# Merge and output projection: merge inputs one merge ahead, w_o by column halves, four token tiles at once

## The chip, the cores and the metric

The kernel runs as one launch on one core of one Trainium2 chip. The metric is the device time in microseconds, the median of three runs. Engines are named as in the profile: PE (matrix), DVE (vector), ACT (scalar), POOL (GpSimd), SP (which issues most DMAs). A difference of 0.2% (about 5 us) is what a measurement of this kernel can tell from none.

## The reference

One encoder block on 1024 tokens of width 1024 in float32: adaptive norm, an input projection, an attention branch and a state-space (SSD) branch, a gated merge, an output projection and a feed-forward block. The part that the change touches is

```python
merged = sigmoid(g_attn) * (attn @ w_attn_out) + sigmoid(g_ssd) * (ssd @ w_ssd_out)   # ssd is RMS-normed, D_INNER = 2048
x = x + gate1 * (merged @ w_o)                                                        # 1024 x 1024
h2 = rms_norm(x, norm2_w) * (1.0 + scale2) + shift2
```

## The kernel before

Each float32 factor is split into a high and a low part (`split`: ACT casts the high part, DVE subtracts to get the low part), and a product is three matmuls of 128 x 128 by 128 x 512 for each block of 128 along the contraction (high by high, high by low, low by high). Every engine works through a fixed list of instructions in order; the order is set by a scheduler when the kernel is built, and semaphores hold an instruction until its inputs and its buffer are ready.

Two stages matter here. In the first (`p5` in the code), the SSD output is multiplied by `w_so`, one row block `i` of 128 output features at a time. The contraction over 2048 is cut into two halves of 8 blocks: the first half of row blocks 6 and 7 (`HELD = 2`) stays in PSUM (`part`), that of the others was computed earlier and lies in DRAM (`s_d`, read back as `e_s`). So the list of jobs is (6, first), (7, first), then the second half for 6, 7, 0, 1, 2, 3, 4, 5. A job has two units, one for each half of the tokens (512 columns), of 24 matmuls into a PSUM tile `psg` (six buffers). After each unit of a second job comes a merge: it loads the attention output `e_a`, the two gates `e_ga` and `e_gs`, and `e_s`; ACT takes the sigmoid of both gates, POOL multiplies `e_a` by `e_ga` and `e_gs` by the norm `rbc`, DVE adds `psg` to `e_s` (this frees the PSUM buffer), multiplies by `e_gs`, adds `e_a`, and the sum is split into `mh` (ACT) and `ml` (DVE). All four input tiles have two buffers (`bufs=2`). The weights `wraw`, `whi`, `wlo` of a job have two buffers too, so they are loaded and split one job ahead. The merges are named here by row block and half, in their order (6,0), (6,1), (7,0), ... (5,0), (5,1).

In the second stage (`p6`), `w_o` is loaded as eight row blocks of 512 KB (`woraw`, four buffers, so that the last four are loaded only when the first four are split), split into `woh` and `wol`, which take the buffers of the SSD operands `g2h`/`g2l` (tag "mrg") that the last job still reads. Then, for each of eight tiles of 128 tokens and each half of the 1024 columns, 24 matmuls over the blocks k = 0 to 7 add into a PSUM tile `pso` (tag "ps2", four buffers that lie where the `psg` buffers lay), DVE multiplies by `gate1` and adds `x`, and ACT takes the sum of squares. The weights of the feed-forward part (`wop` splits) are prepared in between.

Of the kernel before, what the change touches and what calls it, by code (L numbers as in the profile page):

```python
# [89 lines left out]
def block(ctx: ExitStack, tc: tile.TileContext, ia, out, upto=99, dbg=None):  # L90
# [1154 lines left out]
    def load_wo():  # L1245
        raw = wop.tile([P, D], F32, name="woraw", tag="woraw", bufs=4)
        k = len(wo_raw)
        dma(raw, w_o[k * P:(k + 1) * P, :])
        wo_raw.append(raw)

    g2hi, g2lo = mrg_tiles("g2")
    with tc.tile_pool(name="p5", bufs=1, reuse_waits="tile") as p5, \
# [3 lines left out]
        order = list(range(KT - HELD, KT)) + list(range(KT - HELD))  # L1256
# [37 lines left out]
        for n, (i, second) in enumerate(jobs):  # L1294
# [25 lines left out]
    whi, wlo = mrg_tiles("wo")  # L1320
# [27 lines left out]
    with tc.tile_pool(name="p6", bufs=1, reuse_waits="tile") as p6:  # L1348
        gate1 = p6.tile([P, D], F32, name="gate1")
        dma(gate1, g_d[0].partition_broadcast(P))  # L1350
        for k in range(KT):
            if k >= 4:
                load_wo()
            for half in range(2):
                split(whi[k][half], wlo[k][half], wo_raw[k][:, half * 512:(half + 1) * 512])
# [10 lines left out]

        for t in range(NT):
            th, sl = t // 4, slice((t % 4) * P, (t % 4 + 1) * P)
            x1[t] = p6.tile([P, D], F32, name="x1", tag="x1", bufs=5)
            ss2 = p6.tile([P, 2], F32, name="ss2", tag="ss2", bufs=2)  # L1370
            for n in range(2):
                ns = slice(n * 512, (n + 1) * 512)
                xr = p6.tile([P, 512], F32, name="xr", tag="xr", bufs=2)
                dma(xr, x_in[t * P:(t + 1) * P, ns])
                ps = ps7.tile([P, 512], F32, name="pso", tag="ps2", bufs=4)
                for k in range(KT):
                    T.matmul(ps, mhi[k][th][:, sl], whi[k][n], start=k == 0, stop=False)
                    T.matmul(ps, mhi[k][th][:, sl], wlo[k][n], start=False, stop=False)
                    T.matmul(ps, mlo[k][th][:, sl], whi[k][n], start=False, stop=k == KT - 1)
                tt(V, x1[t][:, ns], ps, gate1[:, ns], ALU.mult)  # L1380
                tt(V, x1[t][:, ns], x1[t][:, ns], xr, ALU.add)
                A.activation(xr, x1[t][:, ns], AF.Square, accum_out=ss2[:, n:n + 1])
# [412 lines left out]
```

## Time and profile before

| what | value |
| --- | --- |
| three runs | 2495.03, 2496.18, 2498.93 us, median 2496.18 us |
| the profiled execution | 2497.45 us, its span 2495.7 us, so 1.75 us lie outside the span |
| granted clock of PE over the span | 0.985 |
| busy share of the span | PE 96%, PE weight load 77%, DVE 69%, ACT 44%, POOL 35% |

A busy share is an average over all stages. The two stages above take the stretch from about 1616 to 1840 us of the span. The clock has two levels, 1.2 and 2.4 GHz, and is given as a share of the higher.

### The profile page before, as it was taken

How to read it: one execution, taken by the hardware profiler on the slowest of the kernel's cores; microseconds unless marked ns; L12 is line 12 of the kernel's file. 1: busy time of each engine (PE TensorE's matmuls, PEld its weight loads, DVE VectorE, ACT ScalarE, POOL GpSimd, SP SyncE). 2: the span in 40 equal slices, each digit the busy share in tenths (PEclk: the TensorE clock that was granted, in tenths of full speed). 3: DMA queues.
4: the chain of work that ended last, by engine and by line, in shares of the span. 5: the costliest groups of instructions: out<-in, count | busy, mean ns of one | idle time of the engine just before them, and what ended most of it. 6: DMA issues, size and time to landing. Idle time of an engine off the chain costs nothing. (4 is left out here: it accounts for less than half of the span.)

```text
span 2495.7 us, 32129 instructions
## 1 busy us (share of the span) xinstructions
PE 2393.4 (96%) x11275; PEld 1916.6 (77%) x11275; DVE 1717.7 (69%) x2293; ACT 1096.2 (44%) x1880; POOL 872.2 (35%) x672
## 2 busy tenths in 40 slices
PE   5899999999999999999899999998998999999999
PEld 5898777888867777777667767776777888788887
DVE  5756346777756666666577797556569887767794
ACT  5454522555556666666333343344232222364430
POOL 2311107666511111110356676424018766114200
PEclk9999999999999999999999999999999999999999
DMA  7654661333531213111676776466315544554522
GB/s 261 192 160 135 203 215 60 92 100 110 178 126 57 85 52 89 56 57 47 207 215 208 216 221 185 146 225 213 112 51 194 189 145 165 214 184 134 156 82 87
DMA packets 282161, 363.36 MB, mean 146 GB/s; under 512 B 33673, under 2 KB 166513, under 8 KB 282001
## 3 DMA queue, kind: packets, MB, share of 16 engines
q1 hardware_dynamic: 209841, 285.22, 36.7%
q10 hardware_dynamic: 72160, 76.11, 9.1%
q8 instruction: 89, 1.46, 0.3%
q14 instruction: 71, 0.58, 0.1%
HBM read 248.18 MB, written 113.06 MB: 145 GB/s over the span
## 5 line engine op out<-in xcount | busy, mean ns | idle before, releaser
L891 DVE TENSOR_REDUCE nm<-pss 128x1 f32<-128x1024 f32 x128 | 156.7, 1225 | 133.6 <-PE pss L889 132.1
L379 PE MATMUL psq<-twl,hh 128*128 128x400 f32 (+1 forms) x512 | 193.0, 379 | 6.2 <-DVE twl L153 6.2
L378 PE MATMUL psq<-twh,hh 128*128 128x400 f32 (+1 forms) x512 | 192.3, 381 | 3.3 <-ACT qkvr L511 1.2
L380 PE MATMUL psq<-twh,hl 128*128 128x400 f32 (+1 forms) x512 | 192.0, 377 | 0.0
L893 ACT ACTIVATE pf<-pss,nm 128x1024 f32<-128x1024 f32 x128 | 143.2, 1119 | 101.7 <-PE pst L904 99.0
L153 DVE TENSOR_TENSOR pl<-pst,ph 128x512 fp32r<-128x512 f32 x256 | 167.9, 683 | 27.8 <-ACT ph L167 27.8
L904 PEld LDWEIGHTS pst<-masks,pf 128*128 128x128 f32 x1024 | 118.4, 140 | 69.9 <-issue 29.6
L167 ACT CAST ph<-pst 128x512 fp32r<-128x512 f32 x256 | 146.5, 586 | 54.0 <-PE pst L904 40.8
L904 PE MATMUL pst<-masks,pf 128*128 128x128 f32 x1024 | 157.0, 276 | 11.7 <-DVE pl L153 9.7
L1673 PE MATMUL p<-o,o 128*128 128x512 f32 x400 | 155.3, 389 | 0.5 <-DVE o L153 0.5
L1672 PE MATMUL p<-o,o 128*128 128x512 f32 x400 | 153.7, 390 | 1.9 <-DVE ac L153 1.4
L153 POOL TENSOR_TENSOR av<-av,rz 64x512 f32<-64x512 f32 x32 | 41.0, 1283 | 326.2 <-DMA rz<-rz 154.9
L1674 PE MATMUL p<-o,o 128*128 128x512 f32 x400 | 153.7, 389 | 0.0
L713 DVE SCALAR_TENSOR_TENSOR tap<-pad,cwT,tap 128x1024 f32<-128x1024 f32 x96 | 123.4, 1285 | 5.2 <-ACT tap L711 3.8
L167 ACT CAST wop<-ws 128x512 fp32r<-128x512 f32 x116 | 72.0, 622 | 113.0 <-PE pp L1332 70.6
L379 PEld LDWEIGHTS psq<-twl,hh 128*128 128x128 f32 x512 | 98.6, 193 | 18.0 <-DVE twl L153 7.3
L153 POOL TENSOR_TENSOR sl<-sl 128x512 f32<-128x512 f32 x32 | 49.8, 1559 | 178.3 <-DVE o L153 72.3
L378 PEld LDWEIGHTS psq<-twh,hh 128*128 128x128 f32 x512 | 97.9, 192 | 15.6 <-ACT qkvr L511 1.5
L380 PEld LDWEIGHTS psq<-twh,hl 128*128 128x128 f32 x512 | 97.9, 191 | 11.6 <-issue 0.9
L167 ACT CAST o<-sl 128x512 fp32r<-128x512 f32 x92 | 57.0, 624 | 105.0 <-PE p L1674 88.0
L941 PE MATMUL pv<-pl,v 128*64 128x512 f32 x256 | 102.1, 419 | 0.0
L153 DVE TENSOR_TENSOR o<-sl,o 128x512 fp32r<-128x512 f32 x92 | 72.4, 790 | 40.3 <-ACT o L167 40.3
(424 smaller groups left out, 6971.2 us busy)
## 6 DMA issues: line engine op xcount, KB each, us to landing
ar<-r SPq DMA_DIRECT2D x100, 256.0 KB
wada<-in_w_ada_dram SPq DMA_DIRECT2D x48, 512.0 KB
r<-in_w_mlp_dram SPq DMA_DIRECT2D x32, 512.0 KB
sl<-in_w_mlp_dram SPq DMA_DIRECT2D x64, 256.0 KB
r<-in_w_in_dram SPq DMA_DIRECT2D x26, 512.0 KB
r<-ro ACTq DMA_DIRECT2D x52, 256.0 KB
r<-as SPq DMA_DIRECT2D x48, 256.0 KB
xb<-cst ACTq DMA_DIRECT2D x20, 512.0 KB
```

The source lines that it names most:

```text
L153: e.tensor_tensor(out=o, in0=a, in1=b, op=op)
L167: (e_hi or A.copy)(hi, src)
L378: T.matmul(o, hhi[k][half][:, sl], hi[:, k % 2, :n], start=k == 0, stop=False)
L379: T.matmul(o, hhi[k][half][:, sl], lo[:, k % 2, :n], start=False, stop=False)
L380: T.matmul(o, hlo[k][half][:, sl], hi[:, k % 2, :n], start=False, stop=k == KT - 1)
L713: V.scalar_tensor_tensor(out=tap, in0=pad[:, k:k + S], scalar=cwT[:, 24 * k + i:24 * k + i + 1], in1=tap, op0=ALU.mult, op1=ALU.add)
L891: V.tensor_reduce(out=nm, in_=ps, axis=AX.X, op=ALU.max, negate=True)
L893: A.activation(pfs[u], ps, AF.Exp, bias=nm, accum_out=zall[:, u:u + 1])
L904: T.transpose(pt[:, k], pf[:, (hf * 4 + k) * P:(hf * 4 + k + 1) * P], ident)
L1672: T.matmul(ps, a[:, 0, sl], b[0], start=start, stop=False)
L1673: T.matmul(ps, a[:, 0, sl], b[1], start=False, stop=False)
L1674: T.matmul(ps, a[:, 1, sl], b[0], start=False, stop=stop)
```

## The change

It touches the two stages and nothing else. The order of the row blocks gets a name (`WO_ORDER`) and is used for `w_o` too.

- The loads, sigmoids and POOL products of a merge are written one merge ahead (`merge_loads`), and `e_a`, `e_gs`, `e_s` have three buffers; `e_ga` keeps two.
- `w_o` is loaded in 16 tiles of 256 KB, the left column half of all eight blocks first (eight buffers), and is split in that order.
- The left half of the first four token tiles is computed at once, in four PSUM tiles, with the block k outermost for the first six blocks and the last two blocks tile by tile.
- `f0`, which shares the buffers of `woraw`, follows their new shape.

```diff
     def load_wo():
-        raw = wop.tile([P, D], F32, name="woraw", tag="woraw", bufs=4)
-        k = len(wo_raw)
-        dma(raw, w_o[k * P:(k + 1) * P, :])
+        raw = wop.tile([P, 512], F32, name="woraw", tag="woraw", bufs=8)
+        n, j = divmod(len(wo_raw), KT)
+        k = WO_ORDER[j]
+        dma(raw, w_o[k * P:(k + 1) * P, n * 512:(n + 1) * 512])
...
-        def merge(i, half, ps):
+        def merge_loads():
+            if not merges:
+                return
+            i, half = merges.pop(0)
...
-            for nm, src in (("e_a", a_d[i]), ("e_ga", gt_d[i]), ("e_gs", gt_d[8 + i]), ("e_s", s_d[i])):
+            for nm, src, n in (("e_ga", gt_d[i], 2), ("e_a", a_d[i], 3), ("e_gs", gt_d[8 + i], 3), ("e_s", s_d[i], 3)):
...
-                t = p5.tile([P, 512], F32, name=nm, tag=nm, bufs=2)
+                t = p5.tile([P, 512], F32, name=nm, tag=nm, bufs=n)
                 dma(t, src[:, hs])
                 ld.append(t)
-            a, ga, gs = ld[:3]
+            ga, a, gs = ld[:3]
             A.activation(ga, ga, AF.Sigmoid)
             A.activation(gs, gs, AF.Sigmoid)
             tt(G, a, a, ga, ALU.mult)
             tt(G, gs, gs, rbc[:, hs], ALU.mult)
+            ahead.append(ld[1:])
...
+                if (n, half) > (HELD, 0):
+                    merge_loads()
                 for k in range(KT):
...
-        for k in range(KT):
-            if k >= 4:
-                load_wo()
-            for half in range(2):
-                split(whi[k][half], wlo[k][half], wo_raw[k][:, half * 512:(half + 1) * 512])
+        for n in range(2):
+            for j, k in enumerate(WO_ORDER):
+                if n:
+                    load_wo()
+                split(whi[k][n], wlo[k][n], wo_raw[n * KT + j])
...
+        def wo_product(ps, t, n, k):
+            th, sl = t // 4, slice((t % 4) * P, (t % 4 + 1) * P)
+            T.matmul(ps, mhi[k][th][:, sl], whi[k][n], start=k == WO_ORDER[0], stop=False)
+            T.matmul(ps, mhi[k][th][:, sl], wlo[k][n], start=False, stop=False)
+            T.matmul(ps, mlo[k][th][:, sl], whi[k][n], start=False, stop=k == WO_ORDER[-1])
...
+        pss = [ps7.tile([P, 512], F32, name="pso", tag="ps2", bufs=4) for _ in range(4)]
+        for k in WO_ORDER[:-2]:
+            for t in range(4):
+                wo_product(pss[t], t, 0, k)
+        for t in range(4):
+            for k in WO_ORDER[-2:]:
+                wo_product(pss[t], t, 0, k)
+            residual(t, 0, pss[t])
```

**On PE, where the output projection begins**, before the change (the first row is the last matmul of the last merge's unit; `pso_15829` is the first token tile, `woh_0_0` the left half of block 0 of `w_o`):

```order
L1312 MATMUL psg_15685<-g2h_7_1_14744,wlo_15552 128x512
L1377 MATMUL pso_15829<-woh_0_0_15729,mh_0_0_14767 128x512 [waits DVE_49,Activation_49]
L1378 MATMUL pso_15829<-wol_0_0_15745,mh_0_0_14767 128x512 [waits DVE_49]
L1379 MATMUL pso_15829<-woh_0_0_15729,ml_0_0_14768 128x512
L1377 MATMUL pso_15829<-woh_1_0_15731,mh_1_0_14769 128x512 [waits Activation_49]
L1378 MATMUL pso_15829<-wol_1_0_15747,mh_1_0_14769 128x512 [waits DVE_49]
```

and now (`pso_15842` is the second token tile):

```order
L1330 MATMUL psg_15705<-g2h_7_1_14744,wlo_15568 128x512
L1402 MATMUL pso_15841<-woh_0_0_15737,mh_6_0_14779 128x512 [waits DVE_49,Activation_49]
L1403 MATMUL pso_15841<-wol_0_0_15753,mh_6_0_14779 128x512 [waits DVE_49]
L1404 MATMUL pso_15841<-woh_0_0_15737,ml_6_0_14780 128x512
L1402 MATMUL pso_15842<-woh_0_0_15737,mh_6_0_14779 128x512 [waits DVE_49]
L1403 MATMUL pso_15842<-wol_0_0_15753,mh_6_0_14779 128x512
```

Before, every third matmul waits for another block of `w_o`; now twelve in a row use one block, and the fourth matmul waits for DVE: the instruction that its semaphore counts to is the `e_s<-e_s,psg` of the last merge, (5,1), which frees the PSUM buffer that `pso_15842` takes.

**On DVE, the last merges and the splits of w_o**, before the change (the first row reads the PSUM tile of merge (5,0), the last row that of (5,1); the digit behind `wol` is the column half):

```order
1220 L153 TENSOR_TENSOR e_s<-e_s,psg 128x512
1221 L153 TENSOR_TENSOR wol_1_15750<-woraw,woh_1_15734 128x512
1222 L153 TENSOR_TENSOR wol_0_15751<-woraw,woh_0_15735 128x512
1223 L153 TENSOR_TENSOR wol_1_15752<-woraw,woh_1_15736 128x512
1224 L153 TENSOR_TENSOR e_gs<-e_s,e_gs 128x512
1225 L153 TENSOR_TENSOR wol_0_15753<-woraw,woh_0_15737 128x512
1226 L153 TENSOR_TENSOR wol_1_15754<-woraw,woh_1_15738 128x512
1227 L153 TENSOR_TENSOR e_gs<-e_gs,e_a 128x512
1228 L153 TENSOR_TENSOR wol_0_15755<-woraw,woh_0_15739 128x512
1229 L153 TENSOR_TENSOR e_s<-e_s,psg 128x512
```

and now:

```order
1222 L155 TENSOR_TENSOR e_s<-e_s,psg 128x512
1223 L155 TENSOR_TENSOR wol_0_15763<-woraw,woh_0_15747 128x512
1224 L155 TENSOR_TENSOR wol_0_15765<-woraw,woh_0_15749 128x512
1225 L155 TENSOR_TENSOR wol_0_15767<-woraw,woh_0_15751 128x512
1226 L155 TENSOR_TENSOR e_gs<-e_s,e_gs 128x512
1227 L155 TENSOR_TENSOR wol_1_15754<-woraw,woh_1_15738 128x512
1228 L155 TENSOR_TENSOR wol_1_15756<-woraw,woh_1_15740 128x512
1229 L155 TENSOR_TENSOR wol_1_15758<-woraw,woh_1_15742 128x512
1230 L155 TENSOR_TENSOR e_gs<-e_gs,e_a 128x512
1231 L155 TENSOR_TENSOR wol_1_15760<-woraw,woh_1_15744 128x512
1232 L155 TENSOR_TENSOR e_s<-e_s,psg 128x512
```

The splits are now the whole left half and then four of the right half. The same read of merge (4,1) stands at row 1209 before and at row 1211 now, so that the read of (5,1) is the twentieth row behind it before, and the twenty-first now.

**On ACT, two merges near the end**, before the change (numbers tell the tiles apart; `e_gs_15586` belongs to merge (4,0), `e_gs_15628` to (4,1), `e_ga_15670` to (5,0)):

```order
L1282 ACTIVATE e_gs_15586<-e_gs_15586 128x512
L1281 ACTIVATE e_ga_15670<-e_ga_15670 128x512
L167 CAST mh_3_1_14789<-e_gs_15536 128x512
L1282 ACTIVATE e_gs_15628<-e_gs_15628 128x512
L167 CAST mh_4_0_14775<-e_gs_15586 128x512
```

and now (`e_gs_15580` belongs to (4,1), `e_ga_15664` to (5,1), `e_gs_15622` to (5,0)):

```order
L1293 ACTIVATE e_gs_15580<-e_gs_15580 128x512
L1292 ACTIVATE e_ga_15664<-e_ga_15664 128x512
L169 CAST mh_3_1_14789<-e_gs_15486 128x512
L1293 ACTIVATE e_gs_15622<-e_gs_15622 128x512
L169 CAST mh_4_0_14775<-e_gs_15528 128x512
```

The pattern of sigmoids and casts is the same; each sigmoid belongs to a merge that is one later than before.

## Rows read from the trace of the kernel before

**Rows 1.** Windows of the run: busy us (instructions) by engine, granted clock, DMA share.

```profile
core 0: us, PE busy (x) PEld busy (x) DVE busy (x) ACT busy (x) POOL busy (x), PEclk, DMA share, GB/s
1732.40:1738.00 5.60, 0.55 (x2) 0.24 (x2) 4.98 (x6) 3.96 (x9) 2.64 (x2) 0.92 0.32 94
1738.00:1754.00 16.00, 14.15 (x29) 8.88 (x30) 15.12 (x24) 9.01 (x17) 4.56 (x2) 0.50 0.68 223
1765.00:1795.00 30.00, 30.00 (x131) 24.33 (x130) 11.29 (x28) 4.97 (x15) 0.00 (x0) 1.00 0.26 89
1860.00:1867.00 7.00, 6.29 (x16) 4.52 (x16) 7.00 (x9) 2.69 (x5) 4.10 (x4) 0.51 0.01 2
```

**Rows 2.** Timeline of PE, 1700 to 1752: rows with idle time ahead of them.

```profile
1707.50 0.50 PE L1312 MATMUL psg<-g2h,wlo 128*128 128x512 f32 x1 [2.46 <-DVE wlo L153]
...
1719.90 0.50 PE L1310 MATMUL psg<-g2h,whi 128*128 128x512 f32 x1 [1.44 <-ACT whi L167]
...
1721.41 0.50 PE L1312 MATMUL psg<-g2h,wlo 128*128 128x512 f32 x1 [0.77 <-DVE wlo L153]
...
1735.27 0.50 PE L1377 MATMUL pso<-woh,mh 128*128 128x512 f32 x1 [2.90 <-ACT woh L167]
1737.95 0.80 PE L1378 MATMUL pso<-wol,mh 128*128 128x512 f32 x1 [2.19 <-DVE wol L153]
```

**Rows 3.** Timeline of PE, 1854 to 1862: a later wait of its kind.

```profile
1860.62 1.12 PE L1361 MATMUL pst<-masks,x 128*128 128x128 f32 x4 [3.73 <-ACT fa L1365]
```

**Rows 4.** Timeline of DVE, 1660 to 1718: its waits for POOL.

```profile
1672.37 0.69 DVE L153 TENSOR_TENSOR e_gs<-psg,e_gs 128x512 f32<-128x512 f32 x1 [5.64 <-POOL e_gs L153]
...
1682.06 1.77 DVE L153 TENSOR_TENSOR e_gs<-e_s,e_gs 128x512 f32<-128x512 f32 x1 [2.07 <-POOL e_gs L153]
...
1687.15 0.69 DVE L153 TENSOR_TENSOR e_gs<-e_s,e_gs 128x512 f32<-128x512 f32 x1 [1.22 <-POOL e_gs L153]
```

**Rows 5.** Timeline of all engines, 1723 to 1731: one round of a merge's ring.

```profile
1724.75 0.32 SPq L1278 DMA_DIRECT2D e_gs<-gt  x1
...
1728.48 0.63 ACT L1282 ACTIVATE e_gs<-e_gs 128x512 f32<-128x512 f32 x1 [4.48 <-DMA e_gs<-gt]
...
1729.66 1.37 DVE L153 TENSOR_TENSOR ml<-e_gs,mh 128x512 fp32r<-128x512 f32 x1 [2.81 <-ACT mh L167]
```

**Rows 6.** Timeline of all engines, 1651 to 1663: where the first merges start.

```profile
1652.27 0.32 SPq L1278 DMA_DIRECT2D e_a<-a  x1
...
1654.93 1.30 POOL L153 TENSOR_TENSOR e_a<-e_a,e_ga 128x512 f32<-128x512 f32 x1 [5.09 <-DMA e_a<-a]
...
1656.25 0.32 SPq L1278 DMA_DIRECT2D e_ga<-gt  x1
...
1657.26 1.03 ACT L167 CAST whi<-wraw 128x1024 fp32r<-128x1024 f32 x1
...
1658.79 0.63 ACT L1281 ACTIVATE e_ga<-e_ga 128x512 f32<-128x512 f32 x1 [0.50 <-POOL e_gs L153]
...
1660.62 0.50 PE L1312 MATMUL psg<-g2h,wlo 128*128 128x512 f32 x1 [1.09 <-DVE wlo L153]
```

**Rows 7.** Timeline of all engines, 1728 to 1750: DVE between the last reads of `psg`.

```profile
1730.95 0.68 DVE L153 TENSOR_TENSOR e_s<-e_s,psg 128x512 f32<-128x512 f32 x1
...
1734.78 1.36 POOL L153 TENSOR_TENSOR e_gs<-e_gs,rbc 128x512 f32<-128x512 f32 x1 [0.92 <-ACT e_gs L1282]
1734.93 1.76 DVE L153 TENSOR_TENSOR wop<-wraw,wop 128x512 fp32r<-128x512 f32 x1
...
1737.22 1.88 DVE L153 TENSOR_TENSOR wol<-woraw,woh 128x512 fp32r<-128x512 f32 x3
...
1738.52 0.33 SPq L1248 DMA_DIRECT2D woraw<-in_w_o_dram  x1
...
1744.14 1.14 ACT L167 CAST woh<-woraw 128x512 fp32r<-128x512 f32 x2 [3.58 <-DMA woraw<-in_w_o_dram]
...
1748.41 0.67 DVE L153 TENSOR_TENSOR e_s<-e_s,psg 128x512 f32<-128x512 f32 x1
```

More of the change, by code (lines that the diff above doesn't have):

```diff
@@ L1255, in block @@
         part = {}
-        order = list(range(KT - HELD, KT)) + list(range(KT - HELD))
+        order = WO_ORDER
         jobs = [(i, 0) for i in order[:HELD]] + [(i, 1) for i in order]
@@ L1284, in merge @@
             tt(G, gs, gs, rbc[:, hs], ALU.mult)
+            ahead.append(ld[1:])
+        def merge(i, half, ps):
+            a, gs, *es = ahead.pop(0)
             if i in part:
@@ L1314, in block @@
                     norm_rows()
+                    merge_loads()
+                    merge_loads()
                 if second:
                     merge(i, half, ps)
-    whi, wlo = mrg_tiles("wo")
+    whi, wlo = ([t[WO_ORDER.index(k)] for k in range(KT)] for t in mrg_tiles("wo"))
     ps7 = ctx.enter_context(tc.tile_pool(name="ps7", bufs=1, space=PSUM, reuse_waits="tile"))
@@ L1365, in modulated @@
             A.activation(f, ps, AF.Identity, scale=s2[:, k:k + 1], bias=modc[:, 2, k:k + 1])
-        for t in range(NT):
[L1368 to L1374, printed above, removed]
-                ps = ps7.tile([P, 512], F32, name="pso", tag="ps2", bufs=4)
[L1376 to L1382, printed above, removed]
+        ss2s = {}
@@ new lines, in residual @@
+        def residual(t, n, ps):
+            ns = slice(n * 512, (n + 1) * 512)
+            if n == 0:
+                x1[t] = p6.tile([P, D], F32, name="x1", tag="x1", bufs=5)
+                ss2s[t] = p6.tile([P, 2], F32, name="ss2", tag="ss2", bufs=5)
+            xr = p6.tile([P, 512], F32, name="xr", tag="xr", bufs=2)
+            dma(xr, x_in[t * P:(t + 1) * P, ns])
+            tt(V, x1[t][:, ns], ps, gate1[:, ns], ALU.mult)
+            tt(V, x1[t][:, ns], x1[t][:, ns], xr, ALU.add)
+            A.activation(xr, x1[t][:, ns], AF.Square, accum_out=ss2s[t][:, n:n + 1])
@@ L1383, in block @@
+        for t in range(4):
+            for k in WO_ORDER[-2:]:
+                wo_product(pss[t], t, 0, k)
+            residual(t, 0, pss[t])
+        for t in range(NT):
+            for n in range(t < 4, 2):
+                ps = ps7.tile([P, 512], F32, name="pso", tag="ps2", bufs=4)
+                for k in WO_ORDER:
+                    wo_product(ps, t, n, k)
+                residual(t, n, ps)
+            ss2 = ss2s[t]
             dma(x1_d[t], x1[t])
```

12 lines of the change are left out of this document (7 added, 5 removed).

## The prediction

> **What bounds the kernel now.** PE is busy for 96% of the span, so I looked for the stretches where it is not. The waits of PE between 1600 and 1860 us led to six pieces of idle time, and the windows priced them. At the change from the SSD products to the output projection PE idles 2.90 and 2.19 us [rows 2], and in the window that follows, 1738 to 1754, the granted clock is 0.50, its lower level of 1.2 GHz [rows 1]. From 1732.37 (1735.27 less the 2.90) to 1754.4 PE gets through 2 and 29, so 31 matmuls [rows 1]. At full clock a matmul takes 30.00 us / 129 = 0.232 us (131 touch the window, two of them lie over its edges [rows 1]), so 31 are worth 7.2 us of these 22.0: **14.8 us are lost there.** Ahead of it PE waits 2.46, 1.44 and 0.77 us for the weights of the last two jobs [rows 2], 4.67 us, and 1.09 us at the start of the merges [rows 6]. All that this change could give back is 14.8 + 4.67 + 1.09 = 20.6 us, 0.8% of the run.
>
> **Why PE waits: the merges are late.** The order tells what must wait for what, and the timeline of DVE how late it is. The last read of a merge's PSUM tile, that of (5,1), runs at 1748.41, 16 us after PE wrote it; that of (4,1) at 1730.95 [rows 7]. The merges go round a ring: the end of one `ml` frees a gate tile, SP issues a load at 1724.75, ACT has it at 1728.48, then follow a cast and the next `ml` from 1729.66 [rows 5]. With 0.68 us for that `ml`, one round takes 1729.66 + 0.68 - 1724.75 = 5.6 us, and a unit of PE takes 24 x 0.232 = 5.57. The merges never catch up what they lost at their start.
>
> **The change, part by part.**
>
> *Third buffers, loads one ahead.* They don't shorten the ring. ACT still takes the sigmoid of a gate whose tile is freed by the merge before, ahead of the cast of the merge in hand (the third excerpt of the order). They give a head start instead. Where the first merges start, DVE waits for POOL's gate products by 5.64, 2.07 and 1.22 us [rows 4], each time because the gate could be loaded only when one of two tiles came free. With a third, the tile for (7,1) is loaded before that point, and so on: up to 8.9 us.
>
> *What it costs at the start.* Ahead of the first `whi` of job 0, ACT now has two sigmoids of `e_ga`, whose loads hang on POOL: before, `e_a` was loaded at 1652.27, POOL ended at 1654.93 + 1.30 = 1656.2, and an `e_ga` issued at 1656.25 was read at 1658.79, 2.54 us later [rows 6]. Now a second POOL product (1.30) and the load behind it (2.54) come before that cast: 1656.2 + 1.3 + 2.54 + a sigmoid of 0.63 gives 1660.7, so `whi` ends at 1661.7, not 1657.26 + 1.03 = 1658.3. PE waits 3.4 us there. It has four more matmuls to do before it needs `wlo` (0.9 us), so at that row it is later by 1 to 2.6 us; I take 1.9. I charge this in full to the merges too: the head start is 8.9 - 1.9 = **7.0 us**.
>
> *PE up to the last unit.* With merges 7 us earlier the 4.67 us of waits for weights go. PE would reach the output projection at 1732.37 - 4.67 + 1.9 = 1729.6, or about 1732.7 if the 3.4 us at the start also lower the clock: a wait of 3.73 us elsewhere [rows 3] is followed by a window of 7 us at 0.51 [rows 1], in which 0.49 of 6.29 busy us, 3.1 us, is lost.
>
> *The new wait.* Here the gain stops. Twelve matmuls for each block of `w_o` need no quick supply of blocks, but the four token tiles need four PSUM buffers at once. The fourth matmul waits for the `e_s<-e_s,psg` of merge (5,1) (first excerpt), which stands on DVE behind eight splits of the left half and four of the right (second excerpt). Its time: the read of (4,1) moves from 1730.95 to 1723.95, and the one that matters comes 21 rows later. A row takes 0.61 us when DVE runs without a break (three in 1.88, less what overlaps [rows 7]): 12.8 us. Two POOL products of merge (5,1) fall into it; beside one, a subtraction took 1.76, not 0.68 us [rows 7], so 2.2 us for two. That is 1723.95 + 15.0 = 1738.95, and with its own 0.68 us PE starts again at **1739.6**. PE has done three matmuls, waited some 7 to 9 us, and by the row of 3.73 us the clock falls: 3.1 us more.
>
> The Trainium skill, page "SBUF — State Buffer", section "Who interferes with whom", says that a DVE instruction with two SBUF inputs contends with a GpSimd instruction that reads SBUF, and that the loser blocks for the whole instruction. The trace agrees: DVE's 1.76 us end 0.55 us after POOL's 1.36 do [rows 7]. By the rule the two products would cost DVE up to 2.6 us, not 2.2, and nothing where DVE is first.
>
> *The late half of w_o.* The first load of the right half is issued after the first left split, near 1727.6, the fourth near 1730.2. The nearest row is a load of 512 KB, issued at 1738.52 and read at 1744.14, 5.6 us later [rows 7]; a gate's 256 KB took 3.7 [rows 5]. At 5.6 us the fourth is there at 1735.8, cast at 1736.4, and DVE comes to it at 1738.3: hidden, by 2 us. The eight more DMA issues on SP (0.33 us each [rows 7]) stand in this slack too, and are charged nothing; without it they cost 2.6 us.
>
> *After that* PE needs the splits of (5,0) only 75 matmuls (17 us) after its start, the right half later still. In the window 1765 to 1795 DVE is busy for 11.3 of 30 us and PE for all [rows 1], so the moved residual, its two `xr` tiles and the smaller `f0` tiles cost nothing; were that slack gone, each residual would add its two DVE rows, 1.2 us.
>
> **Sum.** Before, 31 matmuls are done at 1754.4. Now three are done when PE starts again at 1739.6, and the other 28 take 6.5 us and 3.1 for the clock: 1749.2. The gain is **5.2 us**. The profiled execution took 2497.45 us, 1.3 more than the median, so 2492.2 there and **2491.0 us** as the median. What PE loses or wins before 1739 does not enter: it waits there in any case.
>
> Bounds: a head start of the whole 8.9 us and 0.61 us a row without POOL puts the restart at 1735.5 and the gain at 9.3 us (2487). A head start of 3 us and rows of 0.76 (between 0.61 and the 17.46 / 20 = 0.87 that DVE took from one read to the other before, idle time included [rows 7]) puts it at 1744.6: no gain, 2496.
>
> **Rivals.**
>
> *The buffer is free in time.* If the merges run level with PE, its wait at the fourth matmul is short and the clock stays up, as it mostly did over the first 2.90 us (0.92 in 1732 to 1738 [rows 1]). A restart at 1732.8 gives 1754.4 - 1732.8 - 6.5 = 15.1 us: 2481; no wait at all 17.6 us: 2479. For it: the excerpt on ACT shows the tiles one merge further on. Against it: a head start of 12 us is needed, and the waits that it can come from are 8.9 us.
>
> *The right half is late.* The loads behind `wol_1` are eight in a row behind a weight of 512 KB. If the fourth lands 5 to 6 us later than my 1735.8, DVE stands still before the read, and PE restarts near 1743 to 1744: gain 0 to 1, 2495 to 2496. The row of 5.6 us speaks for it; against it, the tiles are half as big.
>
> *No head start (slower).* If the two `e_ga` at the front of ACT cost the merges the whole 8.9 us (the ring's first loads stand in a row: `e_a`, `e_ga`, `e_a`, `e_ga`), the read of (4,1) stays at 1730.95. With DVE's 0.87 us a row the restart is 1730.95 + 18.3 + 0.7 = 1749.9, 31 matmuls end at 1759.5, and the kernel is 5.1 us slower: 2501. It turns slower from a restart after 1744.8. Against it: only 1.9 us of delay can be read off the rows.
>
> **Chances.** The sum with its bounds 0.62; the buffer free in time 0.16; the right half late 0.10; no head start 0.12. The range holds the first and the third and reaches a little to either side: 2482 to 2498, with 2487 to 2496 for the likeliest case alone. Faster by over 0.2% (5.0 us, what a measurement of this kernel can tell) are the second and the half of the first with a restart before 1739.8: 0.16 + 0.34 = 0.50. Slower by that much is the fourth, 0.12. The rest, 0.38, is within 0.2%.
>
> **What would show it.** A wait of PE at the second `pso` tile on DVE `e_s`, 6 to 9 us long and ended near 1739, and a clock of 0.50 behind it; no waits on `whi` or `wlo` between 1700 and 1725; a wait of 3 to 4 us on `whi` near 1658; DVE's waits for POOL between 1660 and 1690 gone. It is wrong if that wait is under 3 us (merges level with PE), if DVE waits for `woh` of the right half ahead of the read, or if the read of (4,1) is not about 7 us earlier.

## The result, and the profile after

| | before | after |
| --- | --- | --- |
| median | 2496.31 us (20 runs) | 2501.72 us (20 runs) |
| lowest to highest | 2492.81 to 2502.83 us | 2494.68 to 2506.66 us |
| profiled execution, span | 2497.45, 2495.7 us | 2502.71, 2500.9 us |

The ratio of after to before is 1.0018, with a 95% interval of 1.0012 to 1.0024: slower by some 4.5 us, where 5.2 us faster was forecast.

The waits of PE after the change, 1600 to 1880 us (total, times, longest):

```profile
engine line waited for: us in total, times, longest us
PE pso L1402 <- DVE e_s L155: 8.9, 1, 8.9
PE psg L1328 <- ACT whi L169: 5.2, 2, 4.4
...
PE psg L1330 <- DVE wlo L155: 1.1, 1, 1.1
```

The first line is new in kind, a wait for the last read of a merge's PSUM tile. The second is for weights near the start, where PE waited 1.09 us before [rows 6]. The waits on weights of the last two jobs [rows 2] have shrunk to this 1.1 us and 0.8 of the 5.2. The timeline of PE after the change, with the idle time ahead of each row in brackets, gives their places:

```profile
1608.52 0.66 PE L1159 MATMUL psm<-masks,u 128*128 128x128 f32 x4 [1.44 <-POOL u L155]
...
1666.66 0.80 PE L1328 MATMUL psg<-g2h,whi 128*128 128x512 f32 x1 [4.41 <-ACT whi L169]
...
1740.49 0.49 PE L1402 MATMUL pso<-woh,mh 128*128 128x512 f32 x1 [2.15 <-ACT woh L169]
1741.88 0.50 PE L1403 MATMUL pso<-wol,mh 128*128 128x512 f32 x1 [0.90 <-DVE wol L155]
1742.22 0.39 PE L1404 MATMUL pso<-woh,ml 128*128 128x512 f32 x1
1751.51 0.79 PE L1402 MATMUL pso<-woh,mh 128*128 128x512 f32 x1 [8.90 <-DVE e_s L155]
...
1756.67 0.39 PE L1402 MATMUL pso<-woh,mh 128*128 128x512 f32 x1
...
1866.58 1.12 PE L1381 MATMUL pst<-masks,x 128*128 128x128 f32 x4 [3.72 <-ACT fa L1385]
```

Three matmuls, then 8.90 us of idle time, as the forecast said. The twelve matmuls behind it take 1756.67 - 1751.51 = 5.16 us where 12 x 0.232 = 2.78 would do, so the half clock costs 2.4 us.

Executions do not begin this part of the program at the same time, so I count from its own start, the end of the `psm` wait in the first row (1605.77 before, 1608.52 after), to the end of the wait on `fa` in the last (1860.62 before [rows 3], 1866.58 after). This **stage** took 254.85 us before and 258.06 after: **3.2 us of the loss lie in it**. The 2.75 us by which it starts later are not explained by the change: kernels with and without it start this stage anywhere from 1603.8 to 1609.4.

The windows of the run after (columns as in [rows 1]):

```profile
1738.00:1754.00 16.00, 4.04 (x11) 2.49 (x10) 15.43 (x26) 11.51 (x21) 1.27 (x1) 0.65 0.56 175
1754.00:1767.00 13.00, 13.00 (x53) 10.44 (x52) 3.57 (x6) 0.62 (x1) 0.00 (x0) 0.90 0.36 121
```

In the first PE is busy for 4 of 16 us, DVE for 15.4. The timeline of DVE from the read of (4,1) to that of (5,1) shows with what:

```profile
1736.31 0.68 DVE L155 TENSOR_TENSOR e_s<-e_s,psg 128x512 f32<-128x512 f32 x1
...
1740.47 2.56 DVE L155 TENSOR_TENSOR wol<-woraw,woh 128x512 fp32r<-128x512 f32 x3 [0.57 <-ACT woh L169]
1742.95 0.68 DVE L155 TENSOR_TENSOR ml<-e_gs,mh 128x512 fp32r<-128x512 f32 x1
1743.56 1.28 DVE L155 TENSOR_TENSOR wol<-woraw,woh 128x512 fp32r<-128x512 f32 x2
1744.76 0.68 DVE L155 TENSOR_TENSOR e_s<-e_s,psg 128x512 f32<-128x512 f32 x1
1745.36 1.89 DVE L155 TENSOR_TENSOR wol<-woraw,woh 128x512 fp32r<-128x512 f32 x3
1747.16 0.68 DVE L155 TENSOR_TENSOR e_gs<-e_s,e_gs 128x512 f32<-128x512 f32 x1
1747.77 1.89 DVE L155 TENSOR_TENSOR wol<-woraw,woh 128x512 fp32r<-128x512 f32 x3
1749.57 0.68 DVE L155 TENSOR_TENSOR e_gs<-e_gs,e_a 128x512 f32<-128x512 f32 x1
1750.17 0.68 DVE L155 TENSOR_TENSOR wol<-woraw,woh 128x512 fp32r<-128x512 f32 x1
1750.78 0.68 DVE L155 TENSOR_TENSOR e_s<-e_s,psg 128x512 f32<-128x512 f32 x1
```

Only 0.57 us of idle time stand in these 14.5 us. The read of (4,1) is at 1736.31, not 7 us ahead of the 1730.95 of before [rows 7]. Why, the rows of all engines after the change show, where the first merges run:

```profile
1658.16 0.38 PE L1272 MATMUL psr<-dg,ones 128*128 128x128 f32 x2
...
1663.06 0.63 ACT L1292 ACTIVATE e_ga<-e_ga 128x512 f32<-128x512 f32 x1 [3.94 <-DMA e_ga<-gt]
1663.60 0.57 ACT L1273 COPY rbc<-psr 128x512 f32<-128x512 f32 x1
...
1664.24 2.50 POOL L155 TENSOR_TENSOR e_gs<-e_gs,rbc 128x512 f32<-128x512 f32 x2 [2.10 <-ACT rbc L1273]
...
1665.54 0.69 DVE L155 TENSOR_TENSOR e_gs<-psg,e_gs 128x512 f32<-128x512 f32 x1 [4.54 <-POOL e_gs L155]
...
1668.35 0.68 DVE L155 TENSOR_TENSOR e_gs<-psg,e_gs 128x512 f32<-128x512 f32 x1
...
1668.45 2.12 SPq L182 DMA_DIRECT2D wraw<-in_w_ssd_out_dram  x2
...
1670.16 1.75 POOL L155 TENSOR_TENSOR e_a<-e_a,e_ga 128x512 f32<-128x512 f32 x1 [3.42 <-DVE wlo L155]
...
1671.94 0.34 SPq L1289 DMA_DIRECT2D e_ga<-gt  x1
1672.37 0.86 SPq L1289 DMA_DIRECT2D e_gs<-gt  x2
...
1675.99 0.69 DVE L155 TENSOR_TENSOR e_s<-e_s,psg 128x512 f32<-128x512 f32 x1 [1.55 <-PE psg L1330]
...
1677.59 0.63 ACT L1292 ACTIVATE e_ga<-e_ga 128x512 f32<-128x512 f32 x1 [3.87 <-DMA e_ga<-gt]
1678.24 1.27 ACT L1293 ACTIVATE e_gs<-e_gs 128x512 f32<-128x512 f32 x2
...
1678.95 2.55 POOL L155 TENSOR_TENSOR e_gs<-e_gs,rbc 128x512 f32<-128x512 f32 x2 [7.03 <-ACT e_gs L1293]
...
1680.27 1.77 DVE L155 TENSOR_TENSOR e_gs<-e_s,e_gs 128x512 f32<-128x512 f32 x1 [3.60 <-POOL e_gs L155]
```

The row at 1668.35 is the read of (7,1), the one at 1675.99 that of (0,0). Two waits of DVE for POOL are left. The first, 4.54 us at (7,0), is for the norm `rbc`: PE had written it by 1658.54, but on ACT its copy stood behind an `e_ga` sigmoid that waited for its load, so POOL could start only at 1664.24. The second, 3.60 us at (0,0), is for two `e_gs`. Their sigmoids run without a wait at 1678.24, but the data was not there much earlier: POOL freed an `e_ga` tile at 1671.91, the `e_ga` load was issued at 1671.94 behind two weights of 512 KB and used 5.65 us later, and the two `e_gs` loads, issued at 1672.37 behind it, end by their semaphores at 1678.15 and 1678.80, just ahead of each sigmoid. Together DVE waits 4.54 + 3.60 = 8.1 us for POOL. Before, it waited 13.7: the 8.9 of [rows 4] and a wait that lies just ahead of their window, at (6,1) (timeline of DVE before):

```profile
1658.75 0.69 DVE L153 TENSOR_TENSOR e_gs<-psg,e_gs 128x512 f32<-128x512 f32 x1 [4.74 <-POOL e_gs L153]
```

So **some of the waits went, and a head start did show**: the read of (7,1) comes 59.8 us after the start of the stage, 6.8 us earlier than before (66.6). **It was gone one merge on**: the read of (0,0) is at 67.5, 7.2 us later than before, after a wait of 1.55 us for PE, which is itself late there.

### The profile page after: what moved, and what is told of

It is laid out like the page before. It is cut to its first block, busy times and chain, and to the rows that moved or that the text cites. A ratio compares the mean times of both kernels' runs of the same rounds, so it can differ in the third digit from the quotient of the medians.

```text
span 2500.9 us, 32151 instructions
## 1 busy us (share of the span) xinstructions
PE 2390.1 (96%) x11275; PEld 1916.1 (77%) x11275; DVE 1720.9 (69%) x2293; ACT 1094.7 (44%) x1880; POOL 868.1 (35%) x672
## 5 line engine op out<-in xcount | busy, mean ns | idle before, releaser
L906 PE MATMUL pst<-masks,pf 128*128 128x128 f32 x1024 | 157.0, 276 | 11.7 <-DVE pl L155 9.7
L169 ACT CAST wop<-ws 128x512 fp32r<-128x512 f32 x116 | 71.6, 620 | 112.7 <-PE pp L1352 73.3
L155 POOL TENSOR_TENSOR sl<-sl 128x512 f32<-128x512 f32 x32 | 50.0, 1567 | 178.1 <-DVE o L155 72.6
```

Source lines behind the costliest of these rows:

```text
L155: e.tensor_tensor(out=o, in0=a, in1=b, op=op)
L169: (e_hi or A.copy)(hi, src)
L906: T.transpose(pt[:, k], pf[:, (hf * 4 + k) * P:(hf * 4 + k + 1) * P], ident)
```

## The experiments

One table holds what the texts below use. Times of reads count from the start of the stage; "pace" is the time from the read of (0,1) to that of (4,1), divided by eight merges; "wait" is PE's at a `pso` tile for DVE's `e_s`. The ratio is to before, in runs on the same chip, with its 95% interval.

| kernel | ratio | stage | (0,1) | pace | (4,1) | (5,1) | wait |
| --- | --- | --- | --- | --- | --- | --- | --- |
| before | 1 | 254.9 | 70.7 | 6.81 | 125.2 | 142.6 | none |
| after | 1.0018 [1.0012, 1.0024] | 258.1 | 75.1 | 6.58 | 127.8 | 142.3 | 8.90 |
| wo_only | 1.0020 [1.0011, 1.0029] | 257.6 | 71.4 | 6.60 | 124.2 | 142.3 | 9.33 |
| merge_only | 1.0009 [1.0000, 1.0018] | 255.8 | 75.3 | 6.48 | 127.2 | 142.2 | none (`mh` 2.87) |
| banks | 0.9971 [0.9959, 0.9982] | 245.6 | 75.6 | 6.39 | 126.7 | 141.2 | none |
| wo_banks | 0.9981 [0.9972, 0.9990] | 246.8 | 71.6 | 6.78 | 125.8 | 143.0 | none |
| tilewise | 1.0000 [0.9991, 1.0008] | 255.9 | 75.8 | 6.40 | 127.0 | 141.5 | none (`mh` 3.36) |
| halves_tilewise | 1.0013 [1.0004, 1.0023] | 255.8 | 71.3 | 6.71 | 125.0 | 141.9 | none (`mh` 4.71) |
| wo_gs3 | 1.0012 [1.0003, 1.0020] | 257.0 | 72.6 | 6.39 | 123.7 | 140.6 | 9.47 |
| banks_gs3 | 0.9964 [0.9952, 0.9977] | 244.8 | 70.6 | 6.49 | 122.5 | 139.1 | none |
| banks_ega3 | 0.9960 [0.9945, 0.9975] | 245.4 | 74.8 | 6.40 | 126.0 | 140.7 | none |
| no_ega | 0.9997 [0.9985, 1.0008] | 251.4 | 73.7 | 6.00 | 121.7 | 135.9 | 8.40 |
| no_egs | 1.0003 [0.9993, 1.0013] | 254.6 | 73.5 | 6.17 | 122.9 | 138.4 | 9.67 |
| no_gates | 0.9971 [0.9960, 0.9982] | 247.3 | 70.8 | 5.54 | 115.1 | 130.9 | 9.96 |
| mh_dve | 1.0015 [1.0005, 1.0025] | 256.5 | 76.5 | 6.17 | 125.9 | 141.6 | 9.23 |
| wo_mh | 1.0026 [1.0017, 1.0036] | 257.0 | 71.8 | 6.26 | 121.9 | 142.2 | 7.93 |
| banks_mh | 0.9956 [0.9941, 0.9971] | 245.5 | 76.9 | 5.94 | 124.4 | 141.4 | none |
| gs3_banks_mh | 0.9978 [0.9966, 0.9990] | 248.1 | 70.3 | 6.46 | 122.0 | 142.3 | none |
| right_pool | 1.0004 [0.9993, 1.0015] | 255.6 | 75.9 | 6.43 | 127.3 | 140.5 | 7.55 |
| banks_pool | 0.9973 [0.9964, 0.9983] | 247.1 | 74.9 | 6.64 | 128.0 | 141.2 | none |

Theory A of the first runs was that the third buffers gave no head start, because the `e_ga` sigmoids at the front of ACT hold the first merges back, and that the PSUM buffer of the last merge then stops PE. Rival C called the merge part harmless and put all the loss at the projection; rival B made the PSUM buffer only the first of several late things. Letters in a later expectation belong to its own set.

### Which part: wo_only, merge_only

wo_only is after with the merges of before; merge_only is before with the merges of after.

```diff
wo_only, against after
...
-                t = p5.tile([P, 512], F32, name=nm, tag=nm, bufs=n)
+                t = p5.tile([P, 512], F32, name=nm, tag=nm, bufs=2)
...
-                if (n, half) > (HELD, 0):
-                    merge_loads()
...
merge_only, against after
-        raw = wop.tile([P, 512], F32, name="woraw", tag="woraw", bufs=8)
+        raw = wop.tile([P, D], F32, name="woraw", tag="woraw", bufs=4)
...
```

> The part on w_o alone (column halves, four token tiles at once); the merges and their loads stand as before the change. Theory A (the third buffers gave no head start, because the sigmoids of e_ga at the front of ACT hold the first merges back, and the PSUM buffer of the last merge then stops PE at the start of the projection): the wait of 4.4 us near 1662 is gone, the first merges run at the times of before, and PE still stops at a pso tile on DVE e_s, for 8 to 12 us. PE would restart near 1746 on the clock of before and the time is that of before within 2 us (2494.5 to 2498.5). Rival C (the merge part is harmless, all the loss is at the projection): the time stays at that of the changed kernel, 2500 to 2503.

> The part on the merges alone (loads one merge ahead, third buffers); w_o as before the change. Theory A: the wait of 4 us on whi near 1660 stays, the merges are 2 to 3 us later than before at their end, so the splits of w_o are too, and the kernel is 2 to 5 us slower than before: 2498 to 2501.5. Rival C: the time of before or up to 5 us less, 2491 to 2496.5.

The `w_o` part alone is as slow as after and has the wait, 9.33 us; the merge part alone costs 0 to 1.8 per mille and does not have it. So the wait belongs to the `w_o` part, and the new merges hardly shorten it. Both times came out as rival C had them, 2502.36 and 2496.42 us, and not as theory A.

### The buffer that PE waits for: banks, wo_banks

Three of the four first token tiles take PSUM buffers (tag "ps1") that none of the last three merges reads. wo_banks is the same with the merges of before.

```diff
-        pss = [ps7.tile([P, 512], F32, name="pso", tag="ps2", bufs=4) for _ in range(4)]
+        pss = [ps7.tile([P, 512], F32, name="pso", tag="ps1" if t else "ps2", bufs=4) for t in range(4)]
```

> The whole change, with one edit: three of the four token tiles that are computed at once take PSUM buffers of the tag ps1, which none of the last three merges reads, so that no matmul of the projection waits for the last merge. Theory A: the wait of 8.9 us goes, and with it most of the half clock behind it (3 to 6 us); 10 to 13 us less than the changed kernel, 2489 to 2492. Rival B (the PSUM buffer is only the first of several late things; PE stops at the next block of w_o or at mh and ml of the last merge): less than 4 us are won, 2498 to 2502.

> The part on w_o alone with the same PSUM buffers as in banks; merges as before the change. Theory A: neither the early wait nor the one on the last merge. PE waits 2 to 3 us for the first woh as before and then runs on: the 31 matmuls that were done at 1754.4 before are done near 1743 to 1745, so 9 to 11 us less than before, 2485 to 2488. Rival B: 2493 to 2497.

The boundary of banks in the timeline of PE, and its window:

```profile
1740.04 0.51 PE L1402 MATMUL pso<-woh,mh 128*128 128x512 f32 x1 [1.82 <-ACT woh L169]
1741.68 0.50 PE L1403 MATMUL pso<-wol,mh 128*128 128x512 f32 x1 [1.14 <-DVE wol L155]
1742.01 0.39 PE L1404 MATMUL pso<-woh,ml 128*128 128x512 f32 x1
1742.24 0.39 PE L1402 MATMUL pso<-woh,mh 128*128 128x512 f32 x1
...
1738.00:1754.00 16.00, 13.04 (x55) 10.22 (x55) 15.92 (x26) 11.54 (x21) 1.52 (x1) 1.00 0.53 170
```

The fourth matmul follows at once and the clock stays at 1.00. DVE reads (5,1) at 141.2, hardly earlier than in after, but nobody waits. That one line moves the ratio from 1.0018 to 0.9971, 11.7 us, about the 8.90 + 2.4 us of wait and half clock. wo_banks against wo_only says the same for the merges of before, 0.9981 after 1.0020, though its 2491.06 us lie between theory A and rival B. The cause of the loss is shown: the wait turns a gain of 2.9 per mille into a loss of 1.8.

### The order of token tiles: tilewise, halves_tilewise

tilewise is after with the first four token tiles one after the other; halves_tilewise has the merges of before as well, so only the column halves of `w_o` are left of the change.

```diff
-        pss = [ps7.tile([P, 512], F32, name="pso", tag="ps2", bufs=4) for _ in range(4)]
...
-            for n in range(t < 4, 2):
+            for n in range(2):
```

> The whole change except that the first four token tiles are computed one after the other, all eight blocks of w_o for each, so that only one PSUM buffer is needed at first. Theory A: the wait for the last merge moves from the fourth matmul to the twenty-second (mh of block 5 and then the buffer), PE has done 18 matmuls (4 us) more by then and pays short waits for each block; 2 to 4 us less than the changed kernel, 2497 to 2500. Rival (the order with k outermost hides the supply of w_o and is worth its wait): more than the changed kernel, 2502 to 2506.

> The column halves of `w_o` alone: merges as before the change, all token tiles one after the other. The loads in 16 tiles are hidden by both theories, so it runs as the kernel before: 2494 to 2499, with waits of PE on `woh`/`wol` of 2 to 3 us each at the head of the projection, and no wait of 9 us on `e_s`, since 24 matmuls (5.6 us) and those waits stand between the first and the second tile. If a wait of over 5 us on `e_s` appears, the column halves themselves put the last read late, and the four tiles at once are not what costs.

Without the four tiles at once the loss is gone in tilewise. In halves_tilewise it is not: 1.0013 cannot be told from the 1.0018 of after, and its 2500.10 us are a little above what was expected. Neither waits for `e_s`, as expected: 24 matmuls stand between the first and the second tile. But both wait for ACT's `mh`, 3.36 and 4.71 us, at the twenty-second matmul of the first tile, whose last blocks are those of the last merges: the lateness of the merges is paid there. Why the ratio of halves_tilewise is above that of tilewise, with a stage of the same length, is open; the two intervals overlap.

### More buffers: wo_gs3, banks_gs3, banks_ega3

```diff
wo_gs3 and banks_gs3, against wo_only and wo_banks
-                t = p5.tile([P, 512], F32, name=nm, tag=nm, bufs=2)
+                t = p5.tile([P, 512], F32, name=nm, tag=nm, bufs=3 if nm == "e_gs" else 2)
banks_ega3, against banks
-            for nm, src, n in (("e_ga", gt_d[i], 2), ("e_a", a_d[i], 3), ("e_gs", gt_d[8 + i], 3), ("e_s", s_d[i], 3)):
+            for nm, src, n in (("e_ga", gt_d[i], 3), ("e_a", a_d[i], 3), ("e_gs", gt_d[8 + i], 3), ("e_s", s_d[i], 2)):
```

> The part on w_o as in the change; of the merge part only a third buffer for e_gs (e_a, e_ga and e_s keep two, loads as before), so that the sigmoids of e_gs come ahead of those of e_ga at the first merges. Theory A1 (the head start was right in kind, and two sigmoids of e_ga at the front of ACT took it back): the read of merge (4,1) comes 4 to 6 us earlier than in wo_only, the wait on DVE e_s is shorter by as much, and the time is 2492 to 2498. Rival A2 (the merges are set by the latency of their loads all along, and no third buffer moves them): the wait stays at 9 us and the time at that of wo_only, 2500 to 2504.

> As wo_gs3, with the PSUM buffers of banks, so that no matmul waits for the last merge. Theory A1: neither the wait on whi at the start nor those on wlo and whi near 1705 and 1718; 2 to 5 us less than wo_banks and banks, 2485 to 2488. Rival A2: as wo_banks, 2489 to 2493.

> As banks, with three buffers for e_ga and two for e_s. If the sigmoid of e_ga is late because its buffer hangs on POOL's product of two merges before, the wait of 4.5 us on whi near 1665 goes to under 2 us and the time is 2485 to 2488. If it is the load of e_ga itself, or one more e_ga that takes its place at the front, the wait stays and so does the time of banks, 2488 to 2491.

A third `e_gs` buffer alone gives a head start in wo_gs3, for a while: the read of (7,1) comes 5.8 us earlier than in wo_only (62.0 and 67.8), the end of the `ml` of (0,1) 3.4 us, that of the next merge 3.8. The one after that is at 91.6 and 91.7 us: lost. The read of (4,1) is 0.5 us earlier, not the 4 to 6 of theory A1, and the wait stays, as A2 had it; the 2499.41 us lie between the two. With three buffers for `e_ga` too (banks_ega3) the pace stays at 6.40, the wait of PE on `whi` near the start at 4.34 us, and DVE's waits for POOL at 8.2 us. Its 2485.76 us lie where a kernel without the wait on `whi` was expected, so that wait does not decide the time; the interval overlaps that of banks. Buffers alone do not set the pace.

### The gates left out: no_ega, no_egs, no_gates

```diff
no_ega, against after
...
-            A.activation(ga, ga, AF.Sigmoid)
...
-            tt(G, a, a, ga, ALU.mult)
+            tt(G, a, a, rbc[:, hs], ALU.mult)
...
no_egs, against after
...
-            A.activation(gs, gs, AF.Sigmoid)
...
-            tt(G, gs, gs, rbc[:, hs], ALU.mult)
+            tt(G, gs, a, rbc[:, hs], ALU.mult)
...
```

> Leaves out the attention gate: `e_ga` is neither loaded nor put through the sigmoid, and POOL multiplies `e_a` by `rbc` in its place, so POOL, DVE and the buffers of `e_gs` and `e_s` work as in the changed kernel. Theory A, the pace of the merges is set by the chain `e_a`, POOL, next `e_ga` load, its sigmoid, which stands on ACT ahead of the next `mh`: the merges then go level with PE. The read of (4,1) comes 115 to 120 us after the start of the stage (127.8 in the changed kernel), the wait of PE at the second `pso` tile shrinks from 8.90 to under 3 us, and the time is 2488 to 2493. Theory B, the pace is set by the chain `ml`, next `e_gs` load, its sigmoid, `mh`: the read of (4,1) stays at 125 to 128, the wait at 8 to 9.5 us, and the time at 2496 to 2502. Under both, the 4.41 us wait on `whi` near the start is gone.

> Leaves out the SSD gate: `e_gs` is neither loaded nor put through the sigmoid; POOL fills its tile with `e_a` times `rbc`. Theory B (the chain through `e_gs`): the read of (4,1) comes 115 to 120 us after the start of the stage instead of 127.8, the wait of PE at the second `pso` tile is under 3 us, and the time 2488 to 2493. Theory A (the chain through `e_ga`): read at 125 to 128, wait 8 to 9.5 us, 2496 to 2502; the 4.41 us wait on `whi` near the start stays.

> Leaves out both gates, their loads and sigmoids. If either chain alone can hold the pace (each takes about a unit of PE by itself), only this kernel is quick: read of (4,1) at 112 to 120 us after the start of the stage, no wait of over 3 us at the second `pso` tile, 2486 to 2492. If it too waits 8 to 9 us there, with the read of (4,1) after 125, then neither gate's chain holds the merges back, but DVE's own list does (the rows in front of each read), and both theories fall.

Neither single theory holds: each gate costs part of the pace (6.58 to 6.00 and to 6.17), and without both the merges go at PE's pace: 5.54 us each, against 5.57 for PE's unit. The times, 2496.08 and 2498.20 us with one gate, fit neither theory whole. And the expectation that the wait would go with them fell. In no_gates the read of (5,1) comes 11.4 us earlier than in after, but PE now reaches the projection 11.9 us earlier too, and waits as long (timeline of PE):

```profile
1728.06 0.40 PE L1403 MATMUL pso<-woh,ml 128*128 128x512 f32 x1
1738.41 0.80 PE L1401 MATMUL pso<-woh,mh 128*128 128x512 f32 x1 [9.96 <-DVE e_s L155]
```

Between the two last reads DVE's list took 15.8 us there, while PE's two units take 11.1.

### The cast on DVE: mh_dve, wo_mh, banks_mh, gs3_banks_mh

Open was whether late loads hold the merges up, or the place of `mh` on ACT behind them. One round of after, timeline of ACT and DVE:

```profile
1707.83 0.63 ACT L1293 ACTIVATE e_gs<-e_gs 128x512 f32<-128x512 f32 x1 [3.29 <-DMA e_gs<-gt]
1708.36 0.60 ACT L169 CAST mh<-e_gs 128x512 fp32r<-128x512 f32 x1
1709.00 1.38 DVE L155 TENSOR_TENSOR ml<-e_gs,mh 128x512 fp32r<-128x512 f32 x1 [4.20 <-ACT mh L169]
```

The input of that `mh` was ready at 1704.8 (DVE's idle time of 4.20 begins there). It stood behind the sigmoid of a later merge. So the four kernels put `mh` on DVE.

```diff
-            split(mhi[i][half], mlo[i][half], gs)
+            split(mhi[i][half], mlo[i][half], gs, e_hi=V.tensor_copy)
```

> The changed kernel with the cast `mh` on DVE instead of ACT; all loads, sigmoids and buffers stay. Theory C, a finished merge is held up because its `mh` stands on ACT behind a sigmoid that waits for a later gate: the merges now go at 5.5 to 5.9 us each (6.58 in the changed kernel, from the read of (0,1) to that of (4,1)), the read of (4,1) comes 118 to 123 us after the start of the stage (127.8), and the time is 2492 to 2498. The wait at the second `pso` tile stays at 7 to 10 us, since PE comes there earlier too. Theory D, the loads themselves come too late for each merge, whoever waits for them: 6.4 to 6.7 us a merge, read of (4,1) at 126 to 129, time 2499 to 2504; DVE's own 16 more rows (0.6 us each) could make it worse.

> wo_only (merges of before, two buffers each) with `mh` on DVE. Theory C: 5.6 to 6.0 us a merge (6.60 in wo_only), read of (4,1) at 117 to 121 us (124.2), time 2494 to 2499. Theory D: 6.5 to 6.8 us a merge, read at 124 to 126, time 2500 to 2504.

> banks (no wait for the last merge's PSUM buffer) with `mh` on DVE. Theory C: merges at 5.5 to 5.9 us each, the weights' waits of 1 to 2 us before the projection gone, 2483 to 2487. Theory D: 2488 to 2491, as banks (ratio 0.9971).

> banks_gs3 (merges of before with a third buffer for `e_gs`, w_o part, no wait for the last merge's PSUM buffer) with `mh` on DVE. Theory C: 5.5 to 5.9 us a merge (6.49), 2482 to 2486. Theory D: 2486 to 2490, as banks_gs3 (ratio 0.9964).

Theory C is right in part: the pace falls by 0.41, 0.34 and 0.45 us a merge in the first three, of the 1.0 us by which after lags PE, and not at all in the fourth (6.49 to 6.46). The times do not follow C: mh_dve is as slow as after, wo_mh no better than wo_only, for the read of (5,1) stays at 141.6 and 142.2. banks_mh, 2486.15 us, fits C, though its interval overlaps that of banks; gs3_banks_mh, 2491.76 us, is slower than either theory had it. So the place of `mh` on ACT costs pace in three of the four, but the pace does not decide the time.

### DVE's own list: right_pool, banks_pool

```diff
-                split(whi[k][n], wlo[k][n], wo_raw[n * KT + j])
+                split(whi[k][n], wlo[k][n], wo_raw[n * KT + j], e_lo=G if n else None)
```

> The changed kernel with the subtractions of the right half of w_o on POOL instead of DVE. On DVE exactly four rows between the reads of (4,1) and (5,1) go, the order of the rest stays. Theory E, the read of (5,1) is held by DVE's own list: four rows of 0.61 us are 2.4 us, so it comes at 139.5 to 140.5 us after the start of the stage (142.3 in the changed kernel), the wait at the second `pso` tile shrinks from 8.90 to 6.2 to 7.2 us, and the time is 2497 to 2500; what DVE loses beside POOL's new rows can take part of it. Theory F, an input of merge (5,0) or (5,1) is late and DVE would wait for it in any case: read at 142 to 143, DVE with 2 us of idle time ahead of it, time 2500 to 2504.

> The control: banks (PE does not wait for the read of (5,1)) with the same move. Under theory E nothing is gained, 2487 to 2491 as banks (ratio 0.9971), since nothing waits there for DVE's four rows; POOL's slower subtractions (some 1.4 us each) could make the right half late for PE and cost up to a few us. If it gains 2.4 us or more, DVE's list is worth shortening whatever PE waits for.

The last rows of DVE before the read, and PE's wait, in right_pool:

```profile
1742.94 1.88 DVE L155 TENSOR_TENSOR wol<-woraw,woh 128x512 fp32r<-128x512 f32 x3
1744.75 0.68 DVE L155 TENSOR_TENSOR e_gs<-e_s,e_gs 128x512 f32<-128x512 f32 x1
1745.46 1.64 DVE L155 TENSOR_TENSOR e_gs<-e_gs,e_a 128x512 f32<-128x512 f32 x1
1747.02 0.68 DVE L155 TENSOR_TENSOR e_s<-e_s,psg 128x512 f32<-128x512 f32 x1
...
PE pso L1402 <- DVE e_s L155: 7.6, 1, 7.6
```

Theory E holds (wait 7.55, a little over its 7.2 us; time 2497.36). The four rows are gone, no idle time took their place, and the read of (5,1) follows that of (4,1) by 1747.02 - 1733.81 = 13.2 us instead of 14.5. Of the 2.4 us expected, 1.0 went to one row that took 1.64 instead of 0.68 us beside POOL. The ratio falls from 1.0018 to 1.0004; that is more than the 1.35 us by which the wait is shorter, and the intervals overlap. The control gains nothing, as expected: DVE's list matters where PE waits for its last row, and not where it doesn't.

## Why the prediction was wrong

**Right: the wait and its place.** PE waits at the second `pso` tile for `e_s` of (5,1) after three matmuls, 8.90 us (forecast 7 to 9), and the clock falls behind it (2.4 us, forecast 3.1). From the read of (4,1) to that of (5,1) it took 14.5 us (15.0). The early wait on `whi` was 4.41 us (3.4), by the chain given: POOL's product, a load, a sigmoid, twice; what it cost PE is another matter, below. The late half of `w_o` cost no wait of PE.

**Wrong: the step *third buffers, loads one ahead*, and in it the head start of 7.0 us.** The read of (4,1) was forecast 7.0 us earlier; it came at 127.8 us of the stage instead of 125.2, 2.6 later, so the term is off by 9.6 us. The head start was there at (7,1), 6.8 us, and gone at (0,0). Three things went wrong in the step.

- *PE's delay.* I charged 1.9 us for the two `e_ga` at the front. But the wait of 4.41 us with half the clock behind it put PE 6.3 us behind the kernel before (the 193rd `psg` matmul of the second jobs starts at 82.6 us of the stage, and at 76.3 before), and DVE had to wait for PE at (0,0).
- *ACT's order.* The copy of `rbc` stood behind the first of these `e_ga` sigmoids, for which ACT waited 3.94 us, and POOL's product for (7,0) behind the copy.
- *The loads.* I took DVE's waits for POOL as removed because the tile of the next `e_gs` would be there. With three tiles its load was still issued only when an `ml` had freed one, and it came behind two weights: issue to use took 5.9 us. Of 13.7 us of such waits (the forecast's 8.9 left out the one at (6,1)) 8.1 remain, and a third buffer for `e_ga` too leaves 8.2 (banks_ega3).

What each of the three is worth at (0,1) is not shown. The read of (0,1) is 4.4 us later in after (75.1 against 70.7). All nine kernels with the new merges and both gates have it at 74.8 to 76.9, all eight with the old ones, before among them, at 70.3 to 72.6. The `e_ga` sigmoids can hardly be all of it: no_ega, which has none (POOL multiplies `e_a` by `rbc` there), is at 73.7.

**Wrong: the ring of 5.6 us as the pace.** [Rows 5] show one round, and the sum took 0.68 us for an `ml` that took 1.37 in the row. Over eight merges the trace of before has 6.81 us a merge (read of (0,1) at 1676.5, of (4,1) at 1730.95 [rows 7]) and PE's unit takes 5.57, so the merges keep falling behind, and a head start that is not sustained is lost, as wo_gs3 showed. In after the pace is a little better, 6.58, which makes up 1.8 of the 4.4 us.

**The sum with the measured values.** Restart at 1751.51 - 1608.52 = 143.0 us of the stage. The forecast's break-even, 1744.8, is 139.0. So 4.0 us late, less 0.7 for the cheaper clock: 3.3 us slower, and the stage measured 3.2. The chain from the read of (4,1) to the time was right; its first term was not. (The forecast's 31 matmuls count one twice that lies over the edge of two windows; with 30 the break-even is 0.2 us later.) The outcome is that of the third rival, *no head start*, to which I gave 0.12: 2501 us forecast, 2501.7 measured. That the times agree so well is partly luck: the rival left the read of (4,1) where it was and took 18.3 us from there to the last read, where it came 2.6 us later and the rest took 14.5. Its cause, the two `e_ga` at the front of ACT, is one of the three above.

**Where the expected gain went.** The order with four tiles at once is worth its price only with free PSUM buffers: tilewise 1.0000, after 1.0018, banks 0.9971. And earlier merges would not by themselves have removed the wait: in no_gates the last reads come 11 to 13 us earlier than in after, and PE waits 9.96 us, since it comes earlier as well. Two things make it up. At the read of (4,1) the merges are behind PE (the read comes 6.1 us after PE's last matmul for it in no_gates, 11.6 in after), and from there DVE's list takes 13 to 20 us in these kernels against PE's 11; right_pool, with a list shorter by 1.3 us, waits 1.35 us less. What an earlier last read does give is an earlier restart, as the forecast had it: in no_gates PE restarts at 131.7 us of the stage, 7.3 ahead of the break-even, and the stage is 7.6 us shorter than before.

**Left open:** how the 4.4 us at (0,1) divide, what makes up the rest of the merges' lag (after moving `mh`, 0.4 to 0.7 us a merge), the 1.3 us between the loss in the stage and that in the ratio, and the spread of the start of the stage.

The best versions beat both kernels: banks_mh 0.9956, banks_ega3 0.9960, banks_gs3 0.9964, 9 to 11 us faster than before; their intervals overlap, and what they share is the freed PSUM buffer.

## What to carry to other kernels

When several output tiles are opened at once, list the last reader of each buffer that they take and its place in its engine's list; one of 0.7 us behind twenty others cost 8.9 us, and free buffers were worth more than everything else here. A further buffer helps only if the load into it is issued and lands in time: ask what frees the tile and what is ahead of the load in its queue. On an in-order engine ask what stands behind a wait that you move to its front; here a copy stood behind one of 3.94 us, and PE came 6.3 us late. Read a pace from the first and the last of many rounds, never from one.

## What was unexpected of the hardware

A cast of 128x512 took 0.43 us on DVE, less than the 0.60 us on ACT, but 1.40 us when POOL's products ran, in mh_dve (timeline of DVE):

```profile
1693.14 0.43 DVE L169 CAST mh<-e_gs 128x512 fp32r<-128x512 f32 x1
...
1701.63 1.40 DVE L169 CAST mh<-e_gs 128x512 fp32r<-128x512 f32 x1
```

The Trainium skill, page "SBUF — State Buffer", section "Who interferes with whom", says that a cast, though it has one input, can run in a mode that needs the port pair shared with GpSimd, and then blocks behind it; the trace agrees: each of the two slow ones of sixteen begins while a POOL product runs and ends 0.28 us after it (for the one above, a product of 1.74 us from 1701.01), and one that began ahead of a product took 0.43 us.

The clock stayed low longer than PE's waits suggest. A window of merge_only (columns as in [rows 1]):

```profile
1740.00:1756.00 16.00, 12.13 (x25) 7.35 (x25) 15.60 (x26) 9.62 (x19) 0.38 (x1) 0.50 0.62 200
```

PE waited 2.21 us just ahead of these 16 us, and 0.60, 0.15, 0.16 and 2.87 in them, and the granted clock was 0.50 throughout; in banks, waits of 1.82 and 1.14 us left it at 1.00.
